# Experts in fours, contiguous expert weights, a re-dealt recurrence, a gate by tanh, and large parts first

## The chip, the cores and the metric

The kernel runs on one core of a Trainium2 chip. The metric is the device time of one execution in microseconds, as the median of several runs. The profiled execution is one of them, read by the hardware profiler; its own time is given as its span.

Engines: PE is TensorE (matmul), PEld its weight loads, DVE is VectorE, ACT is ScalarE, POOL is GpSimd, SP is SyncE, which issues most DMAs here. SBUF is the on-chip memory of 128 partitions, PSUM takes what matmuls produce.

## The reference, cut to what matters

Two blocks stand one behind the other. The first is a half-step `h + 0.5 * swiglu(norm(h))`, a mixer of two kinds of attention, and a second half-step. The second has two layers; each has a mixer and then a mixture of experts, with modulation vectors from a condition. Layer 0's mixer is a gated one (gMLP), layer 1's a recurrence (RWKV) that runs over 256 context tokens and then over 256 latent tokens, in both directions. Layer 0's experts serve 512 tokens, layer 1's the 256 latents alone.

```python
def swiglu(x, w_gate, w_up, w_down):
    return (jax.nn.silu(x @ w_gate) * (x @ w_up)) @ w_down

def _wkv_step(S, inp):                      # per direction z, batch b, head h
    r_t, w_t, k_t, v_t, a_t, b_t = inp
    sa = jnp.einsum('zbhvk,zbhk->zbhv', S, a_t)
    S = S * w_t[..., None, :] + sa[..., :, None] * b_t[..., None, :] + v_t[..., :, None] * k_t[..., None, :]
    return S, jnp.einsum('zbhvk,zbhk->zbhv', S, r_t)

def hier_moe(h, w_grp, b_grp, w_exp, b_exp, w_gate, w_up, w_down):
    grp = jnp.argmax(hf @ w_grp + b_grp, axis=-1)           # one of 4 groups
    top_logit, top_idx = lax.top_k(exp_logits_of(grp), 2)   # 2 of its 8 experts
    ...
    out = (jax.nn.silu(xb @ w_gate[e]) * (xb @ w_up[e])) @ w_down[e]   # 1024 -> 512 -> 1024
    return jnp.einsum('tk,tkd->td', weights, y)
```

All is float32. Each layer has 32 experts with three matrices of 2 MB each, so 192 MB per layer are read.

## The kernel before

The program is one list of instructions per engine. A planner that models the engines' times interleaves the instructions of independent parts on each engine; what the code states is the data that each needs. `run` (L1691) calls the stages in turn: `ffn` (L328), `mixer` (L401), `ffn`, `gmlp` (L631), `moe` (L742) for layer 0, `rwkv` (L1106), `moe` for layer 1, `final` (L1665).

**Products of the dense stages.** Float32 operands are split into a large and a small part (`split` L1067 for activations, `wpart` L1077 for weights), and `mm3` (L1098) adds three products: large weight by small activation, large by large, small by large. `ffn` multiplies features times gain; the tokens' norm `r` is applied to the results of gate and up (L350, L351), then Silu on ACT and a product on DVE.

**Experts.** `experts` (L980) goes through the 32 experts in pairs, 16 rounds. `gather` (L905) collects up to 64 tokens per expert into the 128 columns of X by products with selection matrices; gate and up are products with 64 stationary columns of X (`p[64*j:64*j+64]`, L998) and 512 moving columns of the weights; `hidden` (L944) forms the hidden values and transposes them; `output` (L968) is the down product (L1017) and `combine` (L957) adds the weighted results to the tokens. Tokens beyond an expert's 64 slots go to `extra` (L1025), a loop whose count is computed at run time; it isn't entered in this trace. Weights come through SP's queue (L282 for gate and up, L1011 for down) into rings of buffers of 2 MB: a new load waits until the products on the buffer's last content are done. Layer 1's stage has 8 such buffers. In memory a gate or up matrix lies as 1024 rows of 512 floats, so that a partition gets 8 runs of 2 KB; a half of the down matrix gives 4 runs of 2 KB, one DMA of 1 MB to an expert. The router's logits (L784) are products with the router's weights stationary, in two halves of the array, copied (L786), transposed (L789) and added (L791, L792).

**Recurrence.** `rwkv_project` (L1161) makes keys, values, receptances, decays. Then 8 units (4 of the contexts, 4 of the latents; L1143 to L1156), each with 4 heads in both directions, in 4 chunks of 64 tokens. A unit passes `unit_keys` (L1309: decayed keys, removal vectors `BX`, their products), `unit_values` (L1399), `unit_inverse` (L1558: the inverse of each chunk's triangular matrix, 15 rows solved one after the other by two DVE operations each, L1592 and L1593, then two joins on PE), and `unit_steps` (L1412), where the state passes from chunk to chunk: T (L1447, evicted by L1449 and L1450), UV (L1458), the new state (L1473, L1478), and for latents the output (L1487, L1488). The stages of neighbouring units overlap. `rwkv_out` (L1641) runs the last steps beside the output product.

Of the kernel before, what the change touches and what calls it, by code (L numbers as in the profile page):

```python
# [9 lines left out]
F32 = mybir.dt.float32  # L10
# [3 lines left out]
OP = mybir.AluOpType  # L14
# [12 lines left out]
CAP = 64  # L27
LIM = 64
NXB = 16


# ---------------------------------------------------------------- host layout
# [10 lines left out]
def vec_layout(i):  # L43
    """Every per-feature vector as columns of one [128, n] array; feature d sits at row d % 128, column d // 128."""
# [37 lines left out]
def const_layout():  # L82
    """Constants that depend on shapes alone."""
# [24 lines left out]
    add("thr", np.broadcast_to(LIM + CAP * np.arange(NXB)[None, :], (128, NXB)))  # L108
# [8 lines left out]
    at["mixer"] = (off, 0)                # what follows serves the first block's mixer alone  # L117
# [21 lines left out]
def host_arrays(i):  # L139
    """The inputs as the program takes them: moved and cut, never computed on."""  # L140
# [24 lines left out]
    for n in ("gate", "up", "down"):  # L165
        a["moe_" + n] = f[f"moe_w_{n}_2"]
# [53 lines left out]
class K:  # L220
    C = 64

    def __init__(self, tc, ins, outs, vat, cat, dbg=None):
        self.tc, self.nc, self.i, self.o = tc, tc.nc, ins, outs
        self.vat, self.cat, self.dbg = vat, cat, dbg or {}
        self.n = 0

# [4 lines left out]
    def open(self, es):  # L232
# [15 lines left out]
        self.eps = self.cp.tile([128, 4], F32, name="eps")  # L248
        for j, e in enumerate((EPS, 1e-5, 64e-5, 1e-12)):
# [16 lines left out]
    def psum(self, **bufs):  # L266
        """the eight banks shared out among streams of work"""
# [4 lines left out]
    def wbuf(self):  # L272
        """the next weight buffer, of all rings in turn"""
# [4 lines left out]
    def wtile(self, src, k, m):  # L278
        """src: DRAM AP [128, k, m] (or [128, k * m])."""
# [10 lines left out]
    def more_ring(self, n, side="left", before=()):  # L290
        """n weight buffers for the phases inside, used after those that are there before"""
# [4 lines left out]
    # sum of squares over features -> 1 / sqrt(mean + eps), the same on every partition  # L296
# [17 lines left out]
    def rsqrt(self, pool, out, in_, scale, eps_j, key="", bufs=1):  # L314
        """1 / sqrt(in * scale + eps): the table's value y, then a Newton step y (1.5 - 0.5 u y^2)"""
# [11 lines left out]
    # ------------------------------------------------------------ swiglu half-step, feature-major  # L327
# [1407 lines left out]
```

## Time and profile before

| | |
|---|---|
| median of 3 runs | 2869.97 us (2868.59 to 2870.29) |
| span of the profiled execution | 2864.8 us, 43441 instructions |
| busy over the span | PE 2589.3 us (90%), DVE 1491.7 (52%), ACT 933.0 (33%), POOL 314.4 (11%) |
| read from memory | 604.15 MB |

Stages of the profiled execution by the first work of each: first half-step 0 to 285 us, mixer to 490, second half-step to 690, gMLP to 990, router to 1057, layer 0's experts to 1592, the recurrence's projections to 1765, its units to 2302 (keys are made until 2130), second router to 2347, layer 1's experts to 2836, final norm to 2864.8. A busy share is an average of a stage; the waits and the rate of the DMA say which engine the stage follows.

### The profile page before, as it was taken

The page shows a single profiled execution, that of the slowest core. Times are in us where ns is not written, and L with a number is a line of the kernel's source. Part 1 is how long each engine was busy: PE and PEld are TensorE (multiplying, and loading weights), DVE is VectorE, ACT ScalarE, POOL GpSimd, SP SyncE. Part 2 cuts the span into 40 slices and gives each one's busy share as a digit, 9 for nine tenths or more (in the row PEclk, how much of TensorE's full clock was granted, in tenths as well). Part 3 has the DMA queues.
Part 4 walks back from the last instruction along what each step waited for, and adds up shares of the span by engine and source line. Part 5 has one row for each costly group of instructions (what it writes and reads, how often), then busy time and mean ns, then how long its engine had stood idle before and what let it go on. Part 6 is the DMA issues. An engine that isn't in the chain of part 4 may idle for free. (4 is left out here: it accounts for less than half of the span.)

```text
span 2864.8 us, 43441 instructions
## 1 busy us (share of the span) xinstructions
PE 2589.3 (90%) x17524; PEld 1719.8 (60%) x17524; DVE 1491.7 (52%) x3267; ACT 933.0 (33%) x1686; POOL 314.4 (11%) x460
## 2 busy tenths in 40 slices
PE   8998999998999979999999597787799979999987
PEld 7986757997788744433333286666677744333332
DVE  5644855664564453443333686988975452222222
ACT  4433654543442231111110354554443222111111
POOL 0000100000100000000000212556552000000000
PEclk9999979999999989999999799887676879999999
DMA  8688801543222159999999333221111459999996
GB/s 282 239 318 288 288 15 54 212 171 128 99 89 88 45 194 384 370 363 365 362 367 364 103 114 115 64 69 40 35 45 27 136 203 387 386 387 387 386 386 254
DMA packets 339235, 616.64 MB, mean 215 GB/s; under 512 B 29059, under 2 KB 77779, under 8 KB 336467
## 3 DMA queue, kind: packets, MB, share of 16 engines
q1 hardware_dynamic: 337040, 609.66, 59.4%
q10 hardware_dynamic: 1926, 4.13, 0.4%
q8 instruction: 141, 2.31, 0.3%
q14 instruction: 64, 0.52, 0.1%
q0 software_dynamic: 64, 0.02, 0.0%
HBM read 604.15 MB, written 9.60 MB: 214 GB/s over the span
## 5 line engine op out<-in xcount | busy, mean ns | idle before, releaser
L998 PE MATMUL pg<-w,X 128*64 128x512 f32 x2048 | 510.1, 598 | 12.7 <-DMA w<-in_moe_up_dram 9.8
L1083 DVE TENSOR_TENSOR wl<-w,wh 128x1024 fp32r<-128x1024 f32 (+2 forms) x208 | 248.9, 1200 | 166.9 <-ACT wh L1082 165.1
L998 PEld LDWEIGHTS pg<-w,X 128*64 128x64 f32 x2048 | 154.0, 137 | 301.3 <-issue 281.8
L1082 ACT ACTIVATE wh<-w 128x1024 fp32r<-128x1024 f32 (+2 forms) x208 | 215.4, 1040 | 351.2 <-PE ps L1102 259.7
L966 DVE SCALAR_TENSOR_TENSOR Rl<-pc,mods,Rl 128x256 f32<-128x256 f32 x256 | 118.3, 480 | 298.0 <-PE pc L963 296.2
L1017 PE MATMUL py<-w,hT 128*64 128x512 f32 x992 | 231.6, 602 | 7.2 <-ACT hT L954 4.5
L1101 PE MATMUL ps<-xs,wh 128*128 128x272 f32 (+1 forms) x704 | 202.5, 288 | 3.5 <-ACT wh L1082 3.5
L1103 PE MATMUL ps<-xs,wl 128*128 128x272 f32 (+1 forms) x704 | 201.4, 288 | 1.4 <-DVE wl L1083 1.4
L1102 PE MATMUL ps<-xs,wh 128*128 128x272 f32 (+1 forms) x704 | 201.2, 286 | 0.0
L963 PE MATMUL pc<-tk,y 128*128 128x512 f32 (+1 forms) x512 | 139.6, 376 | 17.2 <-DVE Rl L966 8.0
L963 PEld LDWEIGHTS pc<-tk,y 128*128 128x128 f32 x512 | 77.6, 188 | 125.4 <-issue 72.9
L1017 PEld LDWEIGHTS py<-w,hT 128*64 128x64 f32 x992 | 67.4, 137 | 130.5 <-issue 115.1
L949 DVE SCALAR_TENSOR_TENSOR hh<-hh,tw,pg 128x512 f32<-128x512 f32 x32 | 23.9, 747 | 231.7 <-PE pg L998 231.7
L1101 PEld LDWEIGHTS ps<-xs,wh 128*128 128x128 f32 x704 | 134.0, 190 | 8.4 <-ACT wh L1082 4.7
L1103 PEld LDWEIGHTS ps<-xs,wl 128*128 128x128 f32 x704 | 133.4, 190 | 4.4 <-issue 2.5
L1102 PEld LDWEIGHTS ps<-xs,wh 128*128 128x128 f32 x704 | 133.8, 190 | 0.1
L976 ACT ACTIVATE y<-py 128x512 fp32r<-128x512 f32 x62 | 37.0, 597 | 279.1 <-PE py L1017 237.9
L977 DVE TENSOR_TENSOR y<-py,y 128x512 fp32r<-128x512 f32 x62 | 42.6, 687 | 136.8 <-ACT y L976 136.8
L928 ACT ACTIVATE X<-px 128x512 f32<-128x512 f32 x64 | 35.4, 596 | 228.0 <-PE pg L998 214.8
L948 ACT ACTIVATE hh<-pg 128x512 f32<-128x512 f32 x32 | 19.1, 598 | 254.6 <-PE pg L998 254.6
L1102 PE MATMUL ps<-hid,wh 128*128 128x272 f32 (+1 forms) x352 | 100.1, 284 | 0.0
L1103 PE MATMUL ps<-hid,wl 128*128 128x272 f32 (+1 forms) x352 | 100.0, 284 | 0.0
(492 smaller groups left out, 5528.7 us busy)
## 6 DMA issues: line engine op xcount, KB each, us to landing
w<-in_moe_gate_dram SPq DMA_DIRECT2D x64, 2048.0 KB, 9.4
w<-in_moe_up_dram SPq DMA_DIRECT2D x64, 2048.0 KB, 19.7
w<-in_moe_down_dram SPq DMA_DIRECT2D x128, 1024.0 KB, 14.4
w<-in_ada_w_dram SPq DMA_DIRECT2D x24, 2048.0 KB, 9.3
w<-in_w_down_dram SPq DMA_DIRECT2D x16, 1408.0 KB, 6.7
w<-in_w_gate_dram SPq DMA_DIRECT2D x8, 2048.0 KB, 9.0
w<-in_w_up_dram SPq DMA_DIRECT2D x8, 2048.0 KB, 7.8
w<-in_ga_w_in_dram SPq DMA_DIRECT2D x8, 2048.0 KB, 10.7
```

What stands on the lines that cost most here:

```text
L928: nc.scalar.activation(X[:, b * 4:(b + 1) * 4].rearrange("p k s -> p (k s)"), p[:, :4 * width], AF.Copy)
L963: nc.tensor.matmul(p[:, :n], y[j][:rows, k * 128:(k + 1) * 128], o, start=(j == 0), stop=(j == 1))
L966: nc.vector.scalar_tensor_tensor(R[t][:, k], p[:, s], self.mod(l, 5, k, t), R[t][:, k], op0=OP.mult, op1=OP.add)
L976: nc.scalar.activation(y[0][:rows, s], p[:rows], AF.Copy)
L977: nc.vector.tensor_tensor(y[1][:rows, s], p[:rows], y[0][:rows, s], op=OP.subtract)
L998: nc.tensor.matmul(p[64 * j:64 * j + 64], X[:, k, 64 * j:64 * j + 64], W[2 * b + j][:, k], start=(k == 0), stop=(k == KD - 1), skip_group_ ...
L1017: nc.tensor.matmul(p[64 * j:64 * j + 64], hT[:, k, 64 * j:64 * j + 64], Wd[b][:, j, k], start=(k == 0), stop=(k == 3), skip_group_check=True)
L1082: self.nc.scalar.activation(hi, view, AF.Copy)
L1083: self.nc.vector.tensor_tensor(lo, view, hi, op=OP.subtract)
L1101: mm(p, w[0], x[1], start=start, stop=False, skip_group_check=True)
L1102: mm(p, w[0], x[0], start=False, stop=False, skip_group_check=True)
L1103: mm(p, w[1], x[0], start=False, stop=stop, skip_group_check=True)
```

## The change

- **Layer 1's experts in fours.** `CAPS = (64, 32)`: layer 0 keeps pairs with 64 slots, layer 1 takes four experts with 32 slots each to a round, 8 rounds. The run-time loop now serves what exceeds 32 in layer 1. With the inputs of the reference the fullest expert has 53 tokens in layer 0 and 26 in layer 1.
- **Weights laid out by partition.** The host stores gate and up as [128, 4096] per expert (16 KB a partition in one run), and each half of down as [128, 2048] (8 KB); down comes as one DMA of 2 MB to two experts and a half.
- Layer 1's ring of six opens behind the stage's other pool instead of ahead of it.
- **Router:** the tokens are stationary, the 36 logits' weights move; one addition evicts.
- **Keys:** the +1 behind the tanh goes from DVE to ACT; decays are written behind a column of ones, so that no leading column is copied; removal vectors and added keys lie in one tile and are multiplied by the inverse decays with one product.
- **Inverse:** the row-by-row solution of units 0, 2, 4, 6 runs on POOL.
- **Latents' output:** first all products of one tile shape for both directions, then all of the other.
- **Gate by tanh** in both half-steps, and in the first the norm goes into the features ahead of the products (`normed`).
- **Order of `mm3`:** large by large first, throughout.

The diff, cut to its core:

```diff
-CAP = 64
-LIM = 64
+CAPS = (64, 32)
+LARGE_FIRST, SMALL_FIRST = ((0, 0), (0, 1), (1, 0)), ((0, 1), (0, 0), (1, 0))
...
-    for n in ("gate", "up", "down"):
-        a["moe_" + n] = f[f"moe_w_{n}_2"]
+    for n in ("gate", "up"):
+        a["moe_" + n] = f[f"moe_w_{n}_2"].reshape(2, NE, KD, 128, 512).transpose(0, 1, 3, 2, 4).reshape(2, NE, 128, 4096)
+    a["moe_down"] = f["moe_w_down_2"].reshape(2, NE, 4, 128, 2, 512).transpose(0, 1, 4, 3, 2, 5).reshape(2, NE, 2, 128, 2048)
...
-                nc.vector.tensor_scalar(x, h[:, k], self.v(g, k), None, op0=OP.mult)
+                if normed:
+                    nc.vector.scalar_tensor_tensor(x, h[:, k], self.v(g, k), r[:, :n], op0=OP.mult, op1=OP.mult)
+                else:
+                    nc.vector.tensor_scalar(x, h[:, k], self.v(g, k), None, op0=OP.mult)
...
-                    nc.scalar.activation(sg, sg, AF.Silu)
-                    nc.vector.tensor_mul(sg, sg, up)
+                    if normed:
+                        nc.scalar.activation(sg, pg[:, :n], AF.Tanh, scale=0.5)
+                        nc.vector.scalar_tensor_tensor(sg, sg, 1.0, pg[:, :n], op0=OP.add, op1=OP.mult)
+                        nc.vector.tensor_mul(sg, sg, pu[:, :n])
...
-            es.enter_context(self.more_ring(6, before=self.rings if l else ()))
+            if not l:
+                es.enter_context(self.more_ring(6))
...
+            if l:
+                es.enter_context(self.more_ring(6, before=self.rings))
...
-                        r = slice(k % 2 * 64, k % 2 * 64 + 64)
-                        nc.tensor.matmul(p[r, :SEQ], wr[:, k], h[:, k, t * SEQ:(t + 1) * SEQ], start=(k < 2), stop=(k >= KD - 2), skip_group_check=True)
+                        for j in range(2):
+                            c = t * SEQ + j * 128
+                            nc.tensor.matmul(p[j][:, :36], h[:, k, c:c + 128], wr[:, k, :36], start=(k == 0), stop=(k == KD - 1))
...
+        cap = CAPS[l]
+        G = 128 // cap
-            for q in range(NE // 2):
+            for q in range(NE // G):
-                W = [self.wtile(s[2 * q + j], KD, 512) for s in (gate, up) for j in range(2)]
+                W = [[self.wtile(s[G * q + j], KD, 512) for j in range(G)] for s in (gate, up)]
...
+                        for j in range(G):
+                            a = slice(cap * j, cap * j + cap)
+                            nc.tensor.matmul(p[a], X[:, k, a], w[j][:, k], start=(k == 0), stop=(k == KD - 1), skip_group_check=True)
...
+                    for j in range(G * q, G * q + G, 2):
+                        t = self.wbuf()
+                        nc.sync.dma_start(t.rearrange("p (j x) -> p j x", j=2), down[j:j + 2, b].rearrange("j p x -> p j x"))
...
-        mm(p, w[0], x[1], start=start, stop=False, skip_group_check=True)
-        mm(p, w[0], x[0], start=False, stop=False, skip_group_check=True)
-        mm(p, w[1], x[0], start=False, stop=stop, skip_group_check=True)
+        for n, (a, b) in enumerate(self.order):
+            mm(p, w[a], x[b], start=start and n == 0, stop=stop and n == 2, skip_group_check=True)
...
-                            self.unit_inverse(units[n - 1])
+                            self.unit_inverse(units[n - 1], (v, nc.gpsimd)[n % 2])
...
-                v.tensor_scalar(ts, ts, 1.0, None, op0=OP.add)
+                nc.scalar.activation(ts, ts, AF.Identity, bias=un.W1[z][:, 0, 0:1])
+                BX = un.BX[mm, z] = un.near("BX", [128, 4, 2, C], 4)
+                nc.scalar.activation(BX[:, :, z], un.chunks(ta), AF.Identity, bias=self.eps[:, 4:5], scale=-0.5)
+                nc.scalar.activation(BX[:, :, 1 - z], un.chunks(ta)[:, :, back], AF.Identity, bias=un.ka[:, 1, m:m + 1], scale=un.ka[:, 0, m:m + 1])
...
-                    v.tensor_mul(q[:, :, 1:], knv[o, :, 1:], Wv[o, :, :C - 1])
-                    v.tensor_copy(q[:, :, 0:1], knv[o, :, 0:1])
+                    v.tensor_mul(un.CL[mm][0][o, hh, z], knv[o], Wx[o])
...
+                v.tensor_mul(BX[:, :, z], BX[:, :, z], knv)
+                g.tensor_tensor(BX[:, :, 1 - z], BX[:, :, 1 - z], un.chunks(k)[:, d], op=OP.mult)
...
+                v.tensor_mul(BX.rearrange("p c a t -> p (c a t)"), BX.rearrange("p c a t -> p (c a t)"), Wi.rearrange("p c a t -> p (c a t)"))
...
-                            mmul(p[o, cs], CL[mm][1][:, hh, z, s], HV[:, hh, mm * 2 + z], start=True, stop=False, skip_group_check=True)
-                            mmul(p[o, cs], un.LBr[half(z), mm * 2 + hh, s], UV[half(z), z, cs], start=False, stop=True, skip_group_check=True)
+                for mm in range(NM):
+                    for hh in range(2):
+                        cs = slice((mm * 2 + hh) * 64, (mm * 2 + hh + 1) * 64)
+                        for z in range(2):
+                            mmul(p[z][at[z][0], cs], CL[mm][1][:, hh, z, s], HV[:, hh, mm * 2 + z], start=mm + hh == 0, stop=False, skip_group_check=True)
+                for n in range(NM * 2):
+                    cs = slice(n * 64, (n + 1) * 64)
+                    for z in range(2):
+                        mmul(p[z][at[z][0], cs], un.LBr[half(z), n, s], UV[half(z), z, cs], start=False, stop=n == NM * 2 - 1, skip_group_check=True)
...
-            v.tensor_tensor(tv, Ls[:, s, s + 1:].unsqueeze(2).to_broadcast([128, n, s + 1]), Xs[:, s:s + 1, :s + 1].to_broadcast([128, n, s + 1]), op=OP.mult)
-            v.tensor_tensor(Xs[:, s + 1:, :s + 1], Xs[:, s + 1:, :s + 1], tv, op=OP.add)
+            e2.tensor_tensor(tv, Ls[:, s, s + 1:].unsqueeze(2).to_broadcast([128, n, s + 1]), Xs[:, s:s + 1, :s + 1].to_broadcast([128, n, s + 1]), op=OP.mult)
+            e2.tensor_tensor(Xs[:, s + 1:, :s + 1], Xs[:, s + 1:, :s + 1], tv, op=OP.add)
```

## Rows read from the trace of the kernel before

**Rows 1.** Busy time by stage: start:end, length, PE PEld DVE ACT POOL, clock, DMA share, GB/s

```profile
1057.00:1592.00 535.00, 518.04 (x2172) 211.00 (x2172) 202.30 (x526) 71.77 (x124) 0.00 (x0) 1.00 0.97 353
...
1765.00:2130.00 365.00, 279.96 (x4143) 232.39 (x4144) 315.63 (x749) 176.83 (x400) 207.48 (x325) 0.77 0.21 57
2130.00:2302.00 172.00, 155.25 (x1922) 120.88 (x1920) 86.14 (x188) 48.12 (x95) 33.50 (x62) 0.72 0.23 72
...
2347.00:2836.00 489.00, 454.95 (x2047) 184.19 (x2045) 128.72 (x353) 71.13 (x124) 0.00 (x0) 1.00 1.02 377
```

**Rows 2.** Waits inside layer 0's experts (1057 to 1592): total us, times, longest

```profile
PE px L921 <- ACT X L928: 5.5, 8, 0.7
...
SPq L282 <- PE pg L998: 223.0, 49, 11.1
```

**Rows 3.** Waits of PE inside layer 1's experts (2347 to 2836)

```profile
PE pg L998 <- DMA w<-in_moe_up_dram: 9.8, 7, 2.4
```

**Rows 4.** DMA in layer 1's experts, 40 slices of 12.2 us, and their packets

```profile
GB/s 23 373 387 386 387 386 387 387 386 387 386 386 386 386 387 386 387 386 387 387 386 387 386 386 387 385 387 387 386 386 387 386 387 386 387 387 385 387 386 380
DMA packets 91753, 184.34 MB, mean 377 GB/s; under 512 B 1878, under 2 KB 1878, under 8 KB 91731
```

**Rows 5.** DMA from 680 to 700, slices of 0.5 us, and one of its issues

```profile
GB/s 0 12 119 193 303 360 406 414 406 401 410 414 397 381 377 393 389 389 389 381 385 389 389 389 451 438 430 410 442 213 66 0 0 0 0 0 0 0 0 0
...
ws<-in_ga_w_s_dram SPq DMA_DIRECT2D x1, 1024.0 KB, 9.7
```

**Rows 6.** Timeline of PE: start, us, line, tile rows*columns, operands, count

```profile
43.01 1.92 PE L593 MATMUL pa<-w,cs 128*32 128x512 f32 x16
...
1057.04 14.00 PE L998 MATMUL pg<-w,X 128*64 128x512 f32 x64
```

**Rows 7.** Timeline of PE at the end of layer 1's experts

```profile
2829.12 7.08 PE L998 MATMUL pg<-w,X 128*64 128x512 f32 x30 [1.19 <-DMA w<-in_moe_up_dram]
```

**Rows 8.** Groups of DVE in the recurrence (1765 to 2302): shapes, count, busy, mean ns, idle

```profile
L1593 DVE TENSOR_TENSOR Xs<-Xs,tp 128x15 f32<-128x15 f32 (+7 forms) x120 | 36.5, 304 | 3.0
...
L1359 DVE COPY u<-in 64x4 f32<-64x4 f32 x64 | 22.1, 345 | 8.7 <-DMA in<-st 8.3
L1383 DVE TENSOR_TENSOR LBc<-pk,cst 64x512 f32<-64x512 f32 x32 | 22.0, 688 | 4.4 <-PE pk L1382 3.7
L1366 DVE SCALAR_TENSOR_TENSOR b<-ta,in 128x256 f32<-128x256 f32 x32 | 20.8, 649 | 0.3
...
L1371 DVE TENSOR_TENSOR BX<-t,Wi 128x256 f32<-128x256 f32 x32 | 17.6, 549 | 0.0
...
L1346 DVE TENSOR_SCALAR ts<-ts 128x256 f32<-128x256 f32 x32 | 13.2, 412 | 4.2 <-ACT ts L1344 4.0
```

**Rows 9.** Timeline of DVE and of POOL from 1938 to 1946

```profile
1940.71 0.22 DVE L1593 TENSOR_TENSOR Xs<-Xs,tp 128x60 f32<-128x60 f32 x1
1940.97 0.75 DVE L1592 TENSOR_TENSOR tp<-Ls,Xs 128x63 f32<-128x63 f32 x1
...
1940.92 1.50 POOL L1389 TENSOR_TENSOR u<-u,cst 64x256 f32<-64x256 f32 x2 [2.09 <-ACT u L1386]
```

**Rows 10.** Groups of POOL and of ACT in the recurrence

```profile
L1466 POOL TENSOR_TENSOR hs<-HV,WC 64x128 f32<-64x128 f32 x112 | 51.4, 477 | 85.3 <-DVE HV L1478 72.7 <-DVE Hst L1478 8.3 <-DVE WC L1353 2.1
...
L1351 ACT ACTIVATE Wi<-cum 128x256 f32<-128x256 f32 x32 | 12.9, 404 | 3.4 <-DVE cum L1348 3.4
```

**Rows 11.** Timeline of PE inside one step of the recurrence

```profile
2273.52 0.69 PE L1447 MATMUL pt<-HV,u 128*64 128x64 f32 x16
...
2277.50 0.33 PE L1488 MATMUL pt<-UV,u 64*64 64x64 f32 x2
2277.76 0.33 PE L1487 MATMUL pt<-HV,u 128*64 128x64 f32 x2
```

**Rows 12.** Timeline of ACT at the start, and of the second router

```profile
20.50 0.49 ACT L321 ACTIVATE rstd<-ps,eps 128x272 f32<-128x272 f32 x1 [0.30 <-PE ps L304]
...
2329.34 0.38 ACT L786 ACTIVATE lp<-ps 128x256 f32<-128x256 f32 x1 [1.65 <-PE ps L784]
```

More of the change, by code (lines that the diff above doesn't have):

```diff
@@ L247, in open @@
         nc.gpsimd.tensor_copy(self.count[:, 1], self.ones)
[L248 to L249 removed]
+        self.eps = self.cp.tile([128, 5], F32, name="eps")
+        for j, e in enumerate((EPS, 1e-5, 64e-5, 1e-12, -0.5)):
             nc.vector.memset(self.eps[:, j:j + 1], e)
@@ L982, in experts @@
         nt = n // 128
-        gate = i["moe_gate"][l].rearrange("e (k p) f -> e p k f", p=128)
-        up = i["moe_up"][l].rearrange("e (k p) f -> e p k f", p=128)
-        down = i["moe_down"][l].rearrange("e (k p) f -> e p k f", p=128)
+        gate, up, down = (i["moe_" + n][l] for n in ("gate", "up", "down"))
+        cap = CAPS[l]
+        G = 128 // cap
         with self.tc.tile_pool(name=self.uid("ex"), bufs=2) as pool:
@@ L1036, in extra @@
                 e = nc.sync.value_load(xinfo[0:1, 0:1], min_val=0, max_val=NE - 1)
-                X = self.gather(pool, ht, ol, nt, CAP)
+                X = self.gather(pool, ht, ol, nt, cap)
                 pg, pu = self.ps("pg"), self.ps("pg")
                 for name, p in (("moe_gate", pg), ("moe_up", pu)):
-                    t = weights(name, e, KD, 512)
+                    t = weights(name, e)
                     for k in range(KD):
-                        nc.tensor.matmul(p[:CAP], X[:, k], t[:, k], start=(k == 0), stop=(k == KD - 1))
+                        nc.tensor.matmul(p[:cap], X[:, k], t[:, k], start=(k == 0), stop=(k == KD - 1))
                 d = []
@@ L1048, in extra @@
                                          start=True, stop=True, skip_group_check=True)
-                    d.append(p[:CAP, :n])
-                o, w = self.takers(pool, d, WB, self.c("slot")[:CAP, 0:1], n, CAP)
-                hT = self.hidden(pool, pg, pu, w, CAP)
-                t = weights("moe_down", e, 4, D)
+                    d.append(p[:cap, :n])
+                o, w = self.takers(pool, d, WB, self.c("slot")[:cap, 0:1], n, cap)
+                hT = self.hidden(pool, pg, pu, w, cap)
+                t = self.wbuf()
+                nc.sync.dma_start(t.rearrange("p (b x) -> p b x", b=2), i["moe_down"][l][bass.ds(e, 1)].rearrange("e b p x -> (e p) b x"))
+                t = t.rearrange("p (b k m) -> p b k m", b=2, k=4)
                 def product(b, p):
                     for k in range(4):
-                        nc.tensor.matmul(p[:CAP], hT[:, k], t[:, k, b * 512:(b + 1) * 512], start=(k == 0), stop=(k == 3))
-                self.combine(R, l, n, self.output(pool, CAP, product), o, CAP)
-                nc.vector.tensor_scalar(ol, ol, -float(CAP), None, op0=OP.add)
+                        nc.tensor.matmul(p[:cap], hT[:, k], t[:, b, k], start=(k == 0), stop=(k == 3))
+                self.combine(R, l, n, self.output(pool, cap, product), o, cap)
+                nc.vector.tensor_scalar(ol, ol, -float(cap), None, op0=OP.add)
                 sh = pool.tile([1, NXB], I32, tag="sh", name=self.uid("sh"))
@@ L1142, in rwkv @@
                 with self.tc.tile_pool(name="sk", bufs=1) as ep, self.psum(ps=1, pk=2, pi=1):
-                    units = [Unit(self, ep, sp, part, u, st=st, lora=lora, hb=hb, ka=ka, Rl=Rl, bon=bon, sg=sgt, Hst=Hst[u], T=T)
+                    W1 = [ep.tile([128, 4, self.C + 1], F32, name=f"W1{z}") for z in range(2)]
+                    for t in W1:
+                        nc.gpsimd.memset(t[:, :, 0:1], 1.0)
+                    units = [Unit(self, ep, sp, part, u, st=st, lora=lora, hb=hb, ka=ka, Rl=Rl, bon=bon, sg=sgt, Hst=Hst[u], T=T, W1=W1)
                              for part in (1, 0) for u in range(4)]
@@ L1334, in unit_keys @@
                 r = un.load(3, mm)
-            kms = None
+            added = []
             for z in range(2):
                 f = self.rev if z else (lambda a: a)
+                back = slice(None, None, -1 if z else 1)
                 p = self.ps()
@@ L1355, in unit_keys @@
+                nc.scalar.activation(Wv, un.chunks(cum), AF.Exp, scale=-he)
+                for a, o in ((z, slice(None)), (1 - z, back)):
+                    nc.scalar.activation(Wi[:, :, a], un.chunks(cum)[:, :, o], AF.Exp, scale=he)
+                v.tensor_copy(un.WC[:, mm, z], Wp[:, :, C])
+                d = slice(None, None, -1 if z else 1)
                 for hh in range(2):
                     o = half(hh)
-                    q = un.CL[mm][0][o, hh, z]
-                    v.tensor_mul(q[:, :, 1:], knv[o, :, 1:], Wv[o, :, :C - 1])
```

124 lines of the change are left out of this document (54 added, 70 removed).

## The prediction

> **What bounds the kernel now.** I read the busy time by stage first [rows 1]. The program is a chain of stages with little overlap between them, so each edit is priced in its own stage. The profiled span is 2864.8 us; the median of the runs is 2869.97, so some 5 us lie around the span, and I sum on 2870 and assume that these 5 us stay.
>
> Both expert stages show TensorE and the DMA near full, and only one of them can be the bound. In layer 0's experts PE is busy 518 of 535 us at full clock [rows 1], its longest waits are for an ACT copy and none of the listed ones is for a DMA, while the DMA queue waits 223 us for PE to give buffers back [rows 2]. That stage is PE's. In layer 1's experts PE is busy 455 of 489 us, its largest wait is for weights [rows 3], and the DMA rate lies at 385 to 387 GB/s in slice after slice [rows 4]: 184.34 MB at 0.387 MB/us are 476 us, so that stage is the DMA's, with PE close behind.
>
> The recurrence has two parts. Up to 2130 DVE is the fullest, 316 of 365 us (86%); from there to 2302 PE is, 155 of 172 (90%), at a mean granted clock of 0.72, so partly at 2.4 and partly at 1.2 GHz [rows 1]. Neither waits long for one thing, so what is taken from the fullest engine shortens these parts by less than its busy time.
>
> **Layer 1's experts: longer rows and groups of four.** The bytes stay. What changes is the run that is contiguous in memory: 2 KB before, 16 KB (gate, up) and 8 KB (down) after. The trace has both lengths next to each other: the matrix of 2 KB rows ends at 385 to 389 GB/s, and the spatial weights behind it (1 MB, rows of 8 KB) run at 451, 438, 430, 410, 442 [rows 5], 434 in the mean. I take 430: 184.34/0.430 = 429 us against 476, a gain of 47. Bounds: 410, the lowest of those slices, gives 450 and a gain of 27; 442 gives 417 and a gain of 59; 387 would give nothing.
>
> The gain is only real if PE can follow, and with pairs it couldn't: 455 us of PE do not fit well into 429. That is what the groups of four are for in the sum. A matmul of 512 columns with 64 columns of weights goes at 14.00/64 = 0.219 us, one with 32 columns at 1.92/16 = 0.120 us [rows 6]. Gate and up are 64 instructions to a pair, in 16 rounds 1024: 224 us become 123; the down product, half as many, 112 become 61. What is done once a round (gather, transposes, combine) is halved as well: (455 - 224 - 112)/2 = 60. PE then has about 244 us for 429 us of DMA. At the end of the stage, what follows the last landing shrinks: the last 30 gate and up instructions take 7.08 us [rows 7], after that about half, and the down product the same; I add 5 us (0 to 7). Together **-52** (-27 to -66).
>
> That the ring opens behind another pool only moves its place in memory: eight buffers serve as before, 0.
>
> Layer 0's experts keep pairs and their 64 columns, so PE's 518 us stay, and a faster DMA only waits longer for PE. **0** (-6 to +6; the cover is PE, which lacks only 17 us of the stage).
>
> **The recurrence, DVE's side.** By groups of DVE [rows 8]: the row-by-row solution is L1593 with 36.5 us and L1592, of the same count and shapes, with about as much: some 70 us, and half the units go to POOL, -35. The added one becomes ACT's, -13. The copies of the leading column go, -22. Of the removal vectors and added keys, three products of 256 stand now, L1366 (20.8), L1371 (17.6) and L1367 between them; in their place come one plain product of 256 (17.6, as L1371) and one of 512 (22, as L1383): 57 become 40, -17. DVE loses 87 of 316 us. ACT gains three activations of 0.40 us [rows 10] to each of 32 passes, 39 us on 177, and stays under DVE. POOL gains 120 of the small operations. No row has one on POOL; the nearest are the 0.30 us that DVE takes for them [rows 8] and POOL's 0.48 us for 64x128 [rows 10]: 36 to 57 us, and I take 36, DVE's, since they have at most 64 columns as POOL's has 128; with the latents' copies (8 of 0.8) POOL goes from 207 to about 250.
>
> Against this stands contention. While POOL multiplies, a DVE operation of 128x63 takes 0.75 us, and 0.22 us for 128x60 just before [rows 9]. The Trainium skill ("SBUF — State Buffer", Who interferes with whom) says the same: a DVE instruction with two SBUF inputs and a GpSimd instruction that reads SBUF share a port under an exclusive lock. By that rule, 36 us more of POOL may cost DVE up to 36 us, and the move of the solution would be worth nothing. The trace agrees with the lock (0.75 against 0.22).
>
> POOL's 42 us more meet a DVE that is busy some 60 to 85% of the time, much of it with both inputs in SBUF: I take 25 us of waiting (0 to 42). So DVE's net loss is 87 - 25 = 62, and 254 us are left for a stretch where PE has 280 [rows 1]. PE then takes over as the fullest engine; I credit half of the 62, **-30** (0 to -60).
>
> **The recurrence, PE's side.** In the latents' output each pair of L1487 and L1488 alternates tile shapes. Starts lie 0.26 us apart for two instructions [rows 11], 0.13 each; sixteen of L1447, of one shape, take 0.69 us [rows 11], 0.04 each. A step has 32 such instructions, 4.2 us; sorted by shape 1.3 to 2. At 16 latent steps some 2.5 us each, 40 us of PE, three quarters of them behind 2130 where PE is at 90%. The step's chain (state, T, UV, next state) doesn't need this output, so only what PE's queue held up comes back: **-30** (-10 to -50). If the planner mixes the shapes again it is 0. Late next is the chain itself, with its evictions on ACT and DVE.
>
> **Small parts.** First half-step: xn now waits for rstd, whose first ACT operation runs at 20.50 [rows 12], and the first product's weights are multiplied at about 13. Its square sums end at about 15; the eight normed features then pass DVE and ACT one after the other at some 0.9 us each, so that the first chunk ends some 6 us later, **+6** (0 to +10). One DVE operation less to a chunk, and Tanh for Silu, lie under PE in both half-steps: 0. The routers lose the copy at 2329.34 [rows 12], the transposes and an addition, some 1.5 us to a group of 256 tokens: **-4** with layer 0's. Large parts first lets a product start before the small part of x is made; PE hardly waits for that: **-2** (0 to -5).
>
> **Sum.** 2870 - 52 + 0 - 30 - 30 + 6 - 4 - 2 = 2758 us, some 3.9% less.
>
> **Rivals.**
> (a) The rate doesn't depend on the row. The 434 is a burst of 1 MB in a quiet stretch, and the 2 KB matrix itself showed 414 at its start [rows 5]; for it speaks the flat 387 of 40 slices [rows 4]. Then the stage keeps 476 us and only its end gets 5 shorter: 2758 + 47 = 2805. The Trainium skill ("DMA: Bandwidth & Descriptors", Where 436 GB/s comes from) has HBM to SBUF bound at about 358 GB/s to a core, which would give this case too; the trace shows 387 held for 476 us, so that bound is not the one at work.
> (b) The recurrence is held by its chain of steps or by the lock, and gives 15 instead of 60: 2803. For it: no single wait in these parts is long; against it: 86% and 90% of one engine.
> (c) The recurrence gives nearly all that the engines lose, 60 + 50: 2708.
> (d) Slower: buffers in fours. All four tiles of a matrix are now needed before its first column group is complete, so they come free together, while eight buffers stand. At full clock a matrix takes 64 x 0.12 = 7.7 us and four tiles land in 8.4/0.43 = 19.5, which fits. If PE, idle over half the stage, falls to 1.2 GHz (0.72 is granted in the recurrence, at 90% busy [rows 1]), it takes 15, and the round's other PE work of some 15 us comes on top of it; then the queue stands still for about 10 us at each matrix, with three of these to a round and eight rounds some 100 to 120 us in all, less the 52: +60 in the stage. With 15 from the recurrence: 2870 + 60 - 15 = 2915. It decides as soon as a matrix plus what stands in front of it exceeds the 19.5 us. Against it: at full clock that sum is 15 at most.
>
> **Chances.** Forecast 0.45, (a) 0.15, (b) 0.2, (c) 0.12, (d) 0.06, and 0.02 for a sum of mishaps near no change. The range reaches from (c) to (a) and (b) with their lower gains: 2700 to 2825. About 0.2% (6 us) is what a measurement of this kernel can tell from no change: faster 0.92, same 0.02, slower 0.06.
>
> **What would show it.** Layer 1's stage at about 435 us with slices near 430 GB/s and PE busy about 245 us there (steps on rate and columns); slices at 387 mean (a), gaps in the DMA row together with a clock under 1.00 mean (d). In the recurrence, DVE about 250 us, POOL 250, L1487 and L1488's successors at 0.05 us apart, and the two parts together near 475 us instead of 537; the parts as long as before with emptier engines mean (b). The first weight product at about 19 us, not 13. The forecast fails at once if layer 0's experts move by more than 10 us, since I hold them for PE's.

## The result, and the profile after

The changed kernel takes 2804.22 us in the median (2788.86 to 2807.84) against 2870.13, a ratio of 0.9755 (95% interval 0.9715 to 0.9794). The profiled execution has a span of 2803.4 us, 61.4 us less than before. By itself this time speaks for the rivals (a) and (b), who gave 2805 and 2803, as much as for the forecast's range; the stages tell them apart.

For the stages I take PE's first or last instruction on the operands that only one stage has (the first product of `us` begins the mixer, the last of `hid` ends the second half-step, the first of the experts' weights with `X` begins the experts, from the first product of the decays' weights to the last of `ys` goes the recurrence, and so on). Times in us, each of one profiled execution:

| stage | before | after | difference | forecast |
|---|---|---|---|---|
| first half-step | 268.1 | 272.4 | +4.3 | +6 |
| attention mixer | 227.0 | 235.9 | +8.9 | 0 |
| second half-step | 190.8 | 190.8 | 0.0 | 0 |
| gMLP | 311.7 | 314.5 | +2.8 | 0 |
| first router | 59.4 | 51.3 | -8.1 | -3 |
| layer 0's experts | 541.8 | 540.2 | -1.6 | 0 |
| projections | 171.6 | 170.3 | -1.3 | 0 |
| recurrence | 539.7 | 523.5 | -16.2 | -60 |
| second router | 37.2 | 33.9 | -3.3 | -1 |
| layer 1's experts, to the end | 517.6 | 470.7 | -46.9 | -52 |

The forecast had another -2 for the order of the split products, with no stage of its own. So the experts came as forecast, and 44 us of what the recurrence was to give are missing.

The busy time of layer 0's experts, the recurrence and layer 1's experts in the changed kernel (stretch, its length, busy us of PE, PEld, DVE, ACT, POOL, granted clock, DMA share, GB/s):

```profile
1064.84:1601.40 536.56, 519.54 (x2187) 211.71 (x2188) 202.29 (x527) 71.78 (x124) 0.00 (x0) 1.00 0.88 352
1775.20:2298.80 523.60, 397.67 (x6112) 333.05 (x6112) 346.41 (x694) 259.67 (x592) 281.90 (x508) 0.77 0.24 74
2332.70:2776.00 443.30, 305.65 (x1764) 91.69 (x1764) 62.44 (x170) 35.70 (x61) 0.00 (x0) 0.82 0.99 416
```

Against [rows 1]: layer 0's line is the same but for the DMA share, as a stage of PE should be. For the recurrence the same stretch of the kernel before is this:

```profile
1770.40:2310.05 539.65, 443.05 (x6112) 360.87 (x6112) 404.44 (x942) 225.81 (x496) 237.94 (x379) 0.76 0.21 61
```

DVE fell from 404 to 346 us, so 58 went, PE from 443 to 398, and POOL rose from 238 to 282. In layer 1's experts PE fell from 455 to 306, and the clock from 1.00 to 0.82. PE's products there of gate and up and of down (shapes, count, busy us, mean ns, idle before):

```profile
L1013 PE MATMUL pg<-w,X 128*32 128x512 f32 x1024 | 193.5, 739 | 114.8 <-DMA w<-in_moe_gate_dram 59.4 <-DMA w<-in_moe_up_dram 51.4 <-SPq L1050 3.9
L1033 PE MATMUL py<-w,hT 128*32 128x512 f32 x480 | 62.9, 596 | 5.7 <-DMA w<-in_moe_down_dram 3.0 <-ACT hT L968 2.2 <-DVE y L991 0.4
```

The DMA in layer 1's experts, 40 slices and the packets, which answers to [rows 4]:

```profile
GB/s 101 426 429 426 426 424 419 428 427 428 426 416 418 428 433 428 419 416 428 425 426 433 417 419 431 428 426 422 419 425 429 429 421 416 431 423 426 428 417 412
DMA packets 16723, 184.38 MB, mean 416 GB/s; under 512 B 1398, under 2 KB 1398, under 8 KB 1398
```

The slices lie at 412 to 433, with a mean of 424 behind the first, where there were 385 to 387 but for the two at either end; the 91753 packets became 16723.

### The profile page after: what moved, and what is told of

It is laid out like the page before. It is cut to its first block, busy times and chain, and to the rows that moved or that the text cites. A ratio compares the mean times of both kernels' runs of the same rounds, so it can differ in the third digit from the quotient of the medians.

```text
span 2803.4 us, 42522 instructions
## 1 busy us (share of the span) xinstructions
PE 2398.2 (86%) x17278; PEld 1612.5 (58%) x17278; DVE 1364.5 (49%) x2836; ACT 926.1 (33%) x1715; POOL 357.7 (13%) x590
## 5 line engine op out<-in xcount | busy, mean ns | idle before, releaser
L1013 PE MATMUL pg<-w,X 128*64 128x512 f32 (+1 forms) x2048 | 450.1, 668 | 114.8 <-DMA w<-in_moe_gate_dram 59.4
L1013 PEld LDWEIGHTS pg<-w,X 128*64 128x64 f32 (+1 forms) x2048 | 117.2, 134 | 407.7 <-issue 242.3
L1119 PE MATMUL ps<-xs,wh 128*128 128x272 f32 (+1 forms) x1408 | 262.2, 287 | 7.0 <-ACT xs L1090 5.5
L1119 PEld LDWEIGHTS ps<-xs,wh 128*128 128x128 f32 x1408 | 220.4, 190 | 11.8 <-ACT xs L1090 6.3
L1033 PE MATMUL py<-w,hT 128*64 128x512 f32 (+1 forms) x976 | 178.0, 597 | 8.6 <-ACT hT L968 4.5
L980 DVE SCALAR_TENSOR_TENSOR Rl<-pc,mods,Rl 128x256 f32<-128x256 f32 x192 | 89.6, 480 | 178.0 <-PE pc L977 177.2
L977 PE MATMUL pc<-tk,y 128*128 128x512 f32 (+1 forms) x384 | 114.7, 399 | 20.5 <-ACT y L990 7.7
L1119 PE MATMUL ps<-hid,wh 128*128 128x272 f32 (+1 forms) x704 | 129.7, 284 | 0.0
L1119 PEld LDWEIGHTS ps<-hid,wh 128*128 128x128 f32 x704 | 109.1, 188 | 4.2 <-issue 4.2
L1033 PEld LDWEIGHTS py<-w,hT 128*64 128x64 f32 (+1 forms) x976 | 48.3, 123 | 103.2 <-issue 85.6
```

What stands on the lines that cost most here:

```text
L977: nc.tensor.matmul(p[:, :n], y[j][:rows, k * 128:(k + 1) * 128], o, start=(j == 0), stop=(j == 1))
L980: nc.vector.scalar_tensor_tensor(R[t][:, k], p[:, s], self.mod(l, 5, k, t), R[t][:, k], op0=OP.mult, op1=OP.add)
L1013: nc.tensor.matmul(p[a], X[:, k, a], w[j][:, k], start=(k == 0), stop=(k == KD - 1), skip_group_check=True)
L1033: nc.tensor.matmul(p[a], hT[:, k, a], Wd[b][j][:, k], start=(k == 0), stop=(k == 3), skip_group_check=True)
L1119: mm(p, w[a], x[b], start=start and n == 0, stop=stop and n == 2, skip_group_check=True)
```

## The experiments

Each kernel is the changed one but for the edit shown. Every length of a stage is from one profiled execution, and where a time is given without a range the kernel was run once. The changed kernel (profiled twice) and three of the others have the same recurrence, and in these five profiles it took 523.5, 526.1, 516.7, 516.8 and 520.4 us, 520.7 in the mean. Two others share another recurrence and took 506.5 and 496.2 us. So a difference of under some 6 us says nothing there, and one of 10 little by itself.

### Who sets the recurrence: the solutions on POOL

The trace of the changed kernel first. POOL from 1907 to 1920 (start, duration, engine, line, operands); L1617 and L1618 are the two operations of a row of the third unit's solution:

```profile
1907.08 0.33 POOL L1617 TENSOR_TENSOR tp<-Ls,Xs 128x48 f32<-128x48 f32 x1
1907.37 0.72 POOL L1411 TENSOR_TENSOR u<-u,cst 64x256 f32<-64x256 f32 x1
1908.06 1.03 POOL L1428 TENSOR_TENSOR kb<-BX,WC 128x512 f32<-128x512 f32 x1
1909.17 1.73 POOL L1411 TENSOR_TENSOR u<-u,cst 64x256 f32<-64x256 f32 x2
1910.86 0.66 POOL L1618 TENSOR_TENSOR Xs<-Xs,tp 128x48 f32<-128x48 f32 x1
1911.49 0.72 POOL L1389 TENSOR_TENSOR BX<-BX,in 128x256 f32<-128x256 f32 x1
1912.18 1.03 POOL L1428 TENSOR_TENSOR kb<-BX,WC 128x512 f32<-128x512 f32 x1
1913.18 0.46 POOL L1617 TENSOR_TENSOR tp<-Ls,Xs 128x55 f32<-128x55 f32 x1
...
1918.64 0.73 POOL L1411 TENSOR_TENSOR u<-u,cst 64x256 f32<-64x256 f32 x1
1919.45 0.29 POOL L1618 TENSOR_TENSOR Xs<-Xs,tp 128x55 f32<-128x55 f32 x1
```

Each needs the one before it, and between these stand several other operations that POOL's list has first: 0.3 to 0.7 us of work, then 2 to 6 us until the next. The third unit's solution went on from 1896 to 1967, 72 us for 30 operations that take 11 together; the fifth unit's took 59 us. The first and the seventh unit's, also on POOL, took 19 us each. On DVE a solution took 9 to 30 us before. And this is who waits for it. The eviction of the third unit's first T on DVE, and then PE's join of the solution's blocks (L1658) and its first use (L1480):

```profile
1950.32 0.43 DVE L1472 COPY T<-pt 64x256 f32<-64x256 f32 x1
```

```profile
1984.52 1.92 PE L1658 MATMUL pi<-XT,G 32*32 32x32 f32 x64 [2.60 <-ACT G L1652]
...
1989.43 0.69 PE L1480 MATMUL pt<-T,X 128*64 128x64 f32 x16
```

T was ready at 1950.8, and the product with the inverse began at 1989.4: 39 us in which this unit's chain of steps stood still. The fifth unit's stood still for 34 us. Between the evictions of T there are two pauses of 50 and 42 us in this trace, behind the third and the fifth unit's first; before, the longest but the first was 26 us.

**All solutions on DVE.**

```diff
-                            self.unit_inverse(units[n - 1], (v, nc.gpsimd)[n % 2])
+                            self.unit_inverse(units[n - 1], v)
```

> The changed kernel with the row-by-row solution of all eight units on DVE. Theory S (the solutions of units 2 and 4 on POOL take 70 and 55 us, since each of their 30 dependent operations queues behind POOL's other work, and the chain of steps waits for them 50 and 41 us): those two pauses between evictions of T vanish (none above 30 us), and the recurrence, 524 us from its first key product to the end of the output product, falls to 455 to 495 us, although DVE gets some 27 us more work; the kernel takes 2740 to 2780 us. Rival L (DVE's load and the shared port set the stage): DVE's 27 us more show, 525 to 550 us, 2805 to 2830 in all. Rival C (the chain of steps by itself sets it): 515 to 530 us, no difference in the total.

Measured: 2790.25 us (2778.50 to 2794.69), a ratio of 0.9691 (0.9646 to 0.9736). The pauses are gone, the longest but the first is 22 us, but the recurrence fell only to 510.5 us and not under 495. Its busy time:

```profile
1762.60:2273.10 510.50, 402.48 (x6112) 335.95 (x6112) 382.41 (x814) 259.17 (x592) 241.77 (x388) 0.78 0.25 77
```

DVE has 382 us here, 36 more than in the changed kernel. So the theory had the place right and the size wrong: without the two pauses, which held the steps for 73 us, the recurrence is only 10 us shorter than the mean of 520.7. That what DVE took over gave the rest back is a guess; no run parts the two.

**POOL for the first and the seventh unit only.**

```diff
+                            self.unit_inverse(units[n - 1], nc.gpsimd if n in (1, 7) else v)
```

> The changed kernel with POOL solving units 0 and 6 alone (no unit's steps wait long behind these two in the changed kernel's trace) and DVE the other six. Theory S: as with all on DVE, 455 to 495 us for the recurrence, within 10 us of that kernel. Rival L: some 13 us more on DVE than in the changed kernel, 520 to 540 us. Rival C: 515 to 530 us.

Measured: 2782.09 us (2775.82 to 2784.76), 0.9652 (0.9607 to 0.9697); the recurrence took 506.5 us, DVE 365. That is 14 us under the changed kernel's mean, although DVE has more to do than there, and above the 495 that the theory gave. Two solutions on POOL are better than four and no worse than none; DVE's load alone would have it the other way round. But that nobody waits long for these two does not hold here. The seventh unit's solution takes 56 us on POOL in this kernel, and its T and the first product with its inverse are these:

```profile
2154.99 0.43 DVE L1472 COPY T<-pt 64x256 f32<-64x256 f32 x1
```

```profile
2183.81 1.12 PE L1480 MATMUL pt<-T,X 128*64 128x64 f32 x16
```

The steps stand still for 28 us, and the recurrence is short all the same. So a pause does not cost its length, and how much of the changed kernel's 10 to 14 us lies in its pauses stays open.

**Solutions cut short, on DVE.** 5 of 15 rows are solved, ten are left out.

```diff
-        for s in range(15):
+        for s in range(5):
```

> The kernel with all solutions on DVE, with 5 of the 15 rows of each solution done and the other ten left out: DVE loses some 50 us of its 382. If DVE sets the pace of the recurrence, it falls from 510.5 to 460 to 490 us; if PE with its lowered clock or the chain of steps sets it, 498 to 515 us.

```profile
1766.40:2231.60 465.20, 385.12 (x6112) 320.23 (x6112) 346.57 (x654) 257.99 (x592) 245.84 (x389) 0.82 0.27 84
```

(2739.55 us in all.) The recurrence fell from 510.5 to 465.2 us, by 45, with 36 us less of DVE. PE has the same instructions and is busy 385 us instead of 402, at a clock of 0.82 instead of 0.78. So with the solutions on DVE neither PE nor the other steps hold the recurrence at 510: the solutions do. The fall is larger than the load that went, so the load is not all; what the earlier inverse and the higher clock have in it this run does not part.

### The keys

**The keys' stage of before**, once with the solutions as in the changed kernel and once with all on DVE. The edit puts the old `unit_keys` in place of the new one.

> The changed kernel with the keys' stage of before: DVE gets 52 us more by the sum of the prediction, ACT 39 us less. If DVE sets the stretch until the last key product, the recurrence gets 15 to 50 us longer than 524 us; if the late solutions on POOL set it (theory S), under 10 us, since DVE idles 29% of the stretch in the changed kernel.

Measured: 529.5 us of recurrence (2826.17 in all, of which the mixer has 255.3, see below): 9 more than the changed kernel's mean, with DVE at 380 us instead of 346.

> The changed kernel with the keys' stage of before and all solutions on DVE: of the recurrence's changes the output's order alone is left. Against the kernel with all solutions on DVE (510.5 us of recurrence, DVE 382 us busy) DVE gets some 34 us more. If DVE sets the pace, 535 to 555 us; if the chain of steps does, 500 to 520 us.

```profile
1767.80:2287.20 519.40, 415.75 (x6112) 346.17 (x6112) 402.72 (x942) 225.97 (x496) 236.63 (x379) 0.75 0.24 74
```

519.5 us (2796.00 in all), again 9 more than its counterpart, with 20 us more of DVE. By the numbers both runs fall into the second case of their expectations (under 10 us longer; 500 to 520, at its edge), so DVE's load does not set the pace alone. Two edits, each with and without the other, make a square of 529.5, 519.5, 520.7 and 510.5 us: the new keys are worth some 9 us with either way of solving, and the solutions on POOL cost some 10 with either keys. Each difference by itself is near the scatter; that they come twice speaks for them. The run has a second use. Of the recurrence's changes it holds the output's order alone, and against 539.7 before it shows 20 us less.

### The latents' output

**Its order as before**, two tile shapes in turn.

```diff
-                for mm in range(NM):
-                    for hh in range(2):
-                        cs = slice((mm * 2 + hh) * 64, (mm * 2 + hh + 1) * 64)
-                        for z in range(2):
+                for z in range(2):
+                    for mm in range(NM):
+                        for hh in range(2):
...
+                            mmul(p[z][at[z][0], cs], CL[mm][1][:, hh, z, s], HV[:, hh, mm * 2 + z], start=True, stop=False, skip_group_check=True)
+                            mmul(p[z][at[z][0], cs], un.LBr[half(z), n, s], UV[half(z), z, cs], start=False, stop=True, skip_group_check=True)
```

> The changed kernel with the latents' output in the order of before (two tile shapes in turn, direction after direction). If the forecast's step on PE holds, the recurrence gets 10 to 50 us longer than the changed kernel's 524 us, most of it behind the last key product; if what was gained there is hidden behind the chain of steps, under 5 us.

PE's two groups of the output, in the kernel before, in this kernel and then in the changed one (shapes, count, busy us, mean ns, idle before):

```profile
L1488 PE MATMUL pt<-UV,u 64*64 64x64 f32 x256 | 50.9, 290 | 1.5 <-ACT UV L1459 1.5
L1487 PE MATMUL pt<-HV,u 128*64 128x64 f32 x256 | 49.5, 286 | 0.0
```

```profile
L1511 PE MATMUL pt<-UV,u 64*64 64x64 f32 x256 | 48.0, 275 | 1.0 <-ACT UV L1481 1.0
L1510 PE MATMUL pt<-HV,u 128*64 128x64 f32 x256 | 47.0, 273 | 0.0
```

```profile
L1509 PE MATMUL pt<-HV,u 128*64 128x64 f32 x256 | 25.7, 258 | 1.0 <-issue 1.0
L1513 PE MATMUL pt<-UV,u 64*64 64x64 f32 x256 | 23.5, 249 | 0.0
```

The same 512 products take 100.4 and 95.0 us in turn and 49.2 sorted. The recurrence is 545.9 us long (2811.51 in all), 20 to 29 more than in the five profiles, and most of it lies behind the last product of the decays' weights: 245 us instead of 223.

### Layer 1's experts: rows and fours apart

**Pairs with the new rows.**

```diff
-CAPS = (64, 32)
+CAPS = (64, 64)
```

> The changed kernel with pairs of 64 slots in layer 1 too: the new rows without the groups of four. The forecast has PE at some 455 us of busy time for pairs, so with 430 GB/s PE becomes the bound and layer 1's experts, from their first product to the end of the kernel 470.7 us in the changed kernel and 517.6 before, take 485 to 505 us, with the granted clock back at 1.00. If the groups of four bring nothing (DMA alone sets the stage), 466 to 475 us.

```profile
2322.50:2800.00 477.50, 454.37 (x2051) 186.63 (x2052) 129.22 (x353) 71.59 (x124) 0.00 (x0) 1.00 0.93 387
```

503.4 us to the end (2827.95 in all), PE busy 454 of the first 477.5 and the clock at 1.00, and none of PE's waits there is for weights: PE is the bound.

**Fours with the old rows.** The host's layout and the transfers are those of before, so that the three matrices have runs of 2 KB again.

```diff
-    for n in ("gate", "up"):
-        a["moe_" + n] = f[f"moe_w_{n}_2"].reshape(2, NE, KD, 128, 512).transpose(0, 1, 3, 2, 4).reshape(2, NE, 128, 4096)
...
+    for n in ("gate", "up", "down"):
+        a["moe_" + n] = f[f"moe_w_{n}_2"]
```

> The changed kernel with the memory layout of before (rows of 2 KB, down by 1 MB), but groups of four in layer 1: if the row length sets the rate, 385 to 388 GB/s in the slices and 512 to 520 us from layer 1's first product to the end, although PE has half its work; layer 0's experts stay within 2 us of 540. If the rate came from the groups (the queue is asked earlier), it stays above 415 GB/s and the time near 471 us.

```profile
GB/s 97 388 386 388 387 386 386 387 386 387 386 387 387 386 387 387 387 386 387 386 387 387 387 386 387 387 386 387 387 386 387 388 386 386 387 386 388 386 387 386
```

386 to 388 GB/s as before, and 511.7 us (2833.78 in all). The four kernels make a square: 517.6 with neither, 503.4 with the rows alone (-14.2), 511.7 with the fours alone (-5.9), 470.7 with both (-46.9). Each edit by itself is stopped by the other's bound; together they give 27 us more than the sum.

### The dense stages

**Small parts first.**

```diff
-        self.order = LARGE_FIRST
+        self.order = SMALL_FIRST
```

(the same in the three other places that set it)

> The changed kernel with the order of before inside each split product (large weight by small activation first). By the forecast large first is worth 0 to 5 us over all dense stages; so each dense stage stays within 3 us of the other kernels' (second half-step 190.8, gMLP 311.9 to 314.5), but for the attention mixer, which took 225 to 255 us in five kernels with the same instructions there and is no measure. If the order itself had cost the mixer time, it comes under 228 us here.

Measured: 2802.04 us (2787.51 to 2812.26), 0.9761 (0.9677 to 0.9844). First half-step 269.6 us, second 190.8, gMLP 311.9, projections 171.3: the order is worth nothing that shows in these. The recurrence, whose output product is a split one too, took 528.9 us, 3 more than the longest of the five; one run does not tell whether that is the order. The mixer took 217.6 us, and 219.7 in the next kernel, which multiplies large parts first: no verdict on the order.

**The norm on the results in the first half-step.**

```diff
-                self.ffn(h, T1, "g_ffn1", i["w1_gate"], i["w1_up"], i["w1_down"], beside, normed=True)
+                self.ffn(h, T1, "g_ffn1", i["w1_gate"], i["w1_up"], i["w1_down"], beside)
```

> The changed kernel with the norm applied to the results again in the first half-step (gate by tanh stays). By the forecast its first weight product goes back from 23 to about 13 us and the first half-step from 270 to 272 us to 263 to 268 us (a gain of 2 to 9). If the late start is made up for later in the stage because weights and not PE set its pace, 268 to 271 us and no difference.

Measured: 2777.44 us (2772.14 to 2794.60), 0.9682 (0.9602 to 0.9762). The first weight product went back from 23.2 to 13.2 us and the stage to 266.5 us, where the kernels with the norm in front have 269.2 to 272.4. Of the 10 us at the start some 3 to 6 are left at its end. What holds the start in the changed kernel, on ACT and on DVE:

```profile
17.71 0.49 ACT L325 ACTIVATE rstd<-ps,eps 128x272 f32<-128x272 f32 x1
...
22.71 0.84 ACT L1090 ACTIVATE xs<-xn 128x272 fp32r<-128x272 f32 x2 [2.25 <-DVE xn L340]
```

```profile
20.69 0.43 DVE L329 SCALAR_TENSOR_TENSOR rstd<-nw,rstd 128x272 f32<-128x272 f32 x1
21.05 1.22 DVE L1100 TENSOR_TENSOR wl<-w,wh 128x1024 fp32r<-128x1024 f32 x1
22.18 0.91 DVE L340 SCALAR_TENSOR_TENSOR xn<-h,vec,rstd 128x272 f32<-128x272 f32 x2
```

rstd's first operation runs at 17.71 and its last on DVE at 20.69; a split of weights stands between it and the first normed feature at 22.18, whose own split follows at 22.71.

### The changed kernel again, and the best of the parts

> The changed kernel itself, on the same chip as the next ones. Its stages have so far shown the same lengths within 3 us in kernels with the same instructions, but for the attention mixer (220 to 255 us) and the recurrence (517 to 526). If that spread is the chip's granted clock and not the schedule, this run gives 217 to 256 and 515 to 528 us again, 2785 to 2815 us in all.

Measured: 2799.71 us (2778.35 to 2806.40), 0.9701 (0.9641 to 0.9762); mixer 245.3, recurrence 520.4, layer 1's experts 470.7.

**Solutions on POOL for two units, half-steps as before.**

```diff
+                            self.unit_inverse(units[n - 1], nc.gpsimd if n in (1, 7) else v)
...
-                        nc.scalar.activation(th, sg, AF.Tanh, scale=0.5)
-                        nc.vector.scalar_tensor_tensor(sg, th, 1.0, sg, op0=OP.add, op1=OP.mult)
+                        nc.scalar.activation(sg, sg, AF.Silu)
...
-                self.ffn(h, T1, "g_ffn1", i["w1_gate"], i["w1_up"], i["w1_down"], beside, normed=True)
+                self.ffn(h, T1, "g_ffn1", i["w1_gate"], i["w1_up"], i["w1_down"], beside)
```

> The changed kernel with POOL solving units 0 and 6 alone, and both half-steps as before (norm on the results, Silu): the two parts of the change that cost time, taken back. From the runs so far 14 us less in the recurrence (507 against 521 in the mean) and 3 to 6 us less in the first half-step, 2775 to 2790 us where the changed kernel takes 2804; if half-steps by tanh were worth something, the second half-step gets longer than its 190.8 us.

Measured: 2762.04 us (2752.85 to 2769.83), 0.9597 (0.9554 to 0.9640), on one chip with the run above: 38 us under the changed kernel's median there, and under what was expected. The stages say where from: recurrence 496.2 us (24 less than in the run above, where the same edit alone had 506.5, so some 10 of it are scatter), first half-step 266.9 (3 less), mixer 221.0 (24 less, by the clock, 0.94 against 0.83, below). The second half-step has 190.7 us with Silu and 190.8 with tanh: the gate itself is worth nothing. It is the fastest of the kernels that do the whole work. In the two profiled executions the distance is 53.5 us, and 24 of them are the mixer's clock and not the edit.

## Why the prediction was right, and where it was not

The time, 2804, lies in the range and on the side forecast, and 46 us above the 2758 of the sum. That it lies in the range owes more to the width of the range, which took in the rivals (a) and (b), than to the sum; the sum holds for the experts and the output's order, and fails in the recurrence on DVE's side. By its steps:

- **Layer 1's experts, -52: right, -47.** The rate was taken as 430 GB/s from a burst of 1 MB; the slices have 424, and the stretch with its start 416. The cover, that PE can follow thanks to the fours, was the other half of the argument, and the square of four kernels shows that it had to be. PE's busy time was put at 244 us and is 306. The down products came as priced (63 us for 61), gate and up took 194 us instead of 123. PE waits 111 of 443 us for gate and up, and the clock fell to 0.82, so partly to 1.2 GHz. Where the weights are there, four products (one to an expert) follow the four before after some 0.42 us at 2.4 GHz and after 0.83 at 1.2, and a third of them started at 1.2: by estimate 36 of the 70 us. The rest is not taken apart. The lowered clock is the condition of rival (d); its consequence did not come, since PE had room: the slices show no gap. The 5 us that I added at the end did not come: from the last landing to the end it is 24 us, and was 25.
- **Rival (a), the rate doesn't depend on the row: refuted** by the kernel with the old rows (387) beside the changed one (424). The Trainium skill's bound of about 358 GB/s from HBM to a core ("DMA: Bandwidth & Descriptors", Where 436 GB/s comes from) is passed by both.
- **Layer 0's experts, 0: right**, 540.2 against 541.8.
- **The recurrence on PE's side, -30: right in kind**, -20 to -25 by two kernels that undo it or hold it alone. The saving in busy time was put at 40 us and is 51 (100.4 to 49.2 in the groups of L1487, L1488 and of their successors); I had 0.04 to 0.06 us per sorted product and it is 0.08 by the changed kernel's rows (8 of L1509 in 0.63 us), but the mixed ones were dearer than 0.13, 0.2 in the mean.
- **The recurrence on DVE's side, -30: wrong, about 0.** Its first half held: DVE was to lose 62 us net and lost 58 (over the whole recurrence, the forecast's for the part up to the last keys), POOL's share of 36 us for the solutions came out at 40. What failed is the step from there to time, "PE then takes over as the fullest engine; I credit half". I priced the move to POOL by busy time and by the lock on the port, and named nobody who waits behind POOL's queue. The solution is a chain of 30 dependent operations; each stands behind other work in POOL's list, so it ended 72 and 59 us after its start, and the steps of two units stood still for it for 39 and 34 us. POOL's list is made by the planner; whether POOL with the chain first in its list would do as well as DVE was not run. Half was too much for the keys as well: 34 and 20 us less of DVE gave 9 us each time. So the keys brought 9 us, and the move to POOL cost about 10 (520.7 with it, 510.5 without, and 529.5 and 519.5 with the old keys; each near the scatter of this stretch), so that nothing was left. How the 10 divide between the pauses and DVE's load stays open. Rival (b) gave 15 us for the whole recurrence, which is what came, but for another reason than either that it named: not the chain of steps by itself, since with all solutions on DVE it got shorter when the solutions did (465 us), and not the lock by much, since the 574 other operations of DVE last 337 us together in the changed kernel and 330 with all solutions on DVE.
- **Small parts.** First half-step +6 forecast, +4 measured, 3 to 6 by the kernel without it; the first weight product came at 23.2 us and not at about 19, since the square sums end at 17.7 and not at about 15 and rstd's five operations on ACT and DVE then last until 21.1; of these 10 us half or more was made up. The routers gave -11 where -4 was forecast: I priced the copy, the transposes and an addition, and put at nothing the products of the logits, on which PE is busy 3 us less in each router (13.2 to 10.1 and 7.0 to 3.9); no run parts the rest. The first router's 59.4 us became 51 to 55 in all kernels. The order of the split products gave nothing, within the 0 to 5 forecast.
- **The mixer, 0 forecast, +9 in the profile:** not the change. See the last section.

Taken together: the sum was 112 us, the profile shows 61; of the 51 missing 44 are the recurrence and 9 the mixer's clock, and the rest nearly cancels.

## What to carry to other kernels

When work moves to an idle engine, price it by the length of its chain and not by its busy time alone: here 30 dependent operations of 11 us took up to 72, since each stood behind other work in the engine's list, and who waits for the last of them has to be named. Then price what the wait is worth: here 73 us of waiting steps went together with a loss of only some 10. Two edits that each lift one of two nearly equal bounds (DMA rows, PE columns) must be made together; tried one by one, each looks worth little. Before a rate is called the DMA's limit, look for a transfer with longer contiguous runs in the same trace.

## What the runs showed of the hardware that was not expected

The granted clock of a stage that isn't changed can move the time as much as the change. The attention mixer has the same 1275 PE instructions in all these kernels (in another order in the one with small parts first); its stretch in three of them, the kernel without the norm in front, the changed one, and the one with the old keys:

```profile
266.50:486.20 219.70, 203.74 (x1275) 147.08 (x1275) 144.69 (x397) 120.64 (x266) 17.14 (x26) 0.95 0.38 134
```

```profile
272.35:508.20 235.85, 222.17 (x1275) 157.85 (x1275) 145.44 (x397) 120.83 (x266) 17.15 (x26) 0.86 0.36 125
```

```profile
270.30:525.60 255.30, 240.85 (x1275) 167.34 (x1275) 145.27 (x397) 120.95 (x267) 17.15 (x26) 0.79 0.33 115
```

At a mean clock of 0.95 it takes 219.7 us, at 0.86 235.9, at 0.79 255.3, with DVE, ACT and POOL equally busy in all three. The changed kernel itself, profiled twice, had 235.9 us at 0.86 and 245.3 at 0.83, so it is not the edits alone. What PE does in the stage is the same by the count of instructions; why it is granted 2.4 GHz for longer in one execution than in another stays open, since none of the runs varied that. With 217.6 to 255.3 us for this one stage, a difference under some 40 us between two single executions of this kernel says nothing before the mixer's length has been looked at.

And the cost of shapes in turn: products of 128x64 and 64x64 tiles that alternate took 95 us where the same products sorted by shape took 49.
